# A two-layer trunk on Trainium2: products in pairs in the MLP steps, another bank group for an output projection's last tiles, and a gather moved by nine matmuls

## The chip, the cores and the metric

The kernel runs on one core of one Trainium2 chip. The core has a matmul engine (PE, TensorE), whose weight loads are shown apart as PEld; a vector engine (DVE); a scalar engine (ACT); GpSimd (POOL); and SyncE (SP), which here only issues DMAs. Matmuls write their sums into PSUM, a memory of eight banks of 128 x 512 floats; everything else lies in SBUF. Each engine works through its own list of instructions in order and waits on semaphores for the others. The metric is device time in microseconds (us).

## What is computed

The reference is a trunk of two layers on 512 tokens of width 1024: a latent-attention mixer (MLA) and its MLP, then a gated linear attention mixer (GLA) and its MLP, and a last RMSNorm:

```python
h = xn @ w_in ...                       # mixer: MLA in layer 0, GLA in layer 1
x = x + mixer(rms_norm(x)) @ w_o        # w_o: 1024 x 1024
hid = jnp.square(jax.nn.relu(xn @ w_up))    # w_up: 1024 x 4096
x = x + hid @ w_down                    # w_down: 4096 x 1024
```

All is float32. GLA normalises each head's output (`rms_norm(o, g_norm)`), multiplies by a gate, and projects with `w_o`.

## The kernel before

**Split products.** A float32 product is made of three matmuls on parts: each operand is split into a high and a low part, and the sum of high x high, high x low and low x high is taken (`mm3`, L112 to L114, and the loops of `up_product` and `down_product`). For a weight, ACT writes the high half (tile `wh`, L104) and DVE subtracts it for the low half (`wl`, L107). Both have four buffers, so a product's halves can be written when the product four earlier has ended.

**The MLP (`mlp`).** The 4096 hidden columns are taken in eight blocks of 512. Each block's two large products are done by a scheme of seven products instead of eight (Strassen's, in Winograd's form): quadrants of weights and of data are added and subtracted first, seven products are made, and their sums are combined. `up_first` makes block 0's hidden values. Then `step(b, ...)`, for b = 0 to 6, makes the seven up products of block b + 1 (`up_product`, L946: 24 matmuls of 256 columns) and the seven down products of block b (`down_product`, L955: 12 matmuls of 512 columns), by turns. With U for up and D for down, and the names used in this document, the order before is

```
U11 D11a U21 D12a  T2 D11b T1 D22 U22 D12 T3 D5 T4 D21
```

T1 to T4 and U.. are up products; `D11b` is the one with minus q11, `D22` that with q22, `D12` that with q12; `D5` and `D21` go through `onto`. The sums lie in four single banks "u" for up products, and in two pairs of banks "d" and "e" for down products. `begun` (L964) copies d into e on ACT, so that a further product can be added there; `onto` copies a running sum into a pair of banks (L976), adds a product and copies it back (L978); `add` (L971) adds a finished pair to a running sum on DVE; `finish` (L849, L850) applies the squared ReLU. After a product, `after(name)` fetches the next weight of a name: SP issues a plain DMA (L933, or L134 for the 1 MB tiles `wraw`), POOL one that accumulates (L935). The order of instructions on each engine follows from the order in which the code records them; a scheduler moves instructions of DVE and ACT within it.

**The output projections (`out_start`, `out_proj`).** Eight tiles m = 0 to 7 of 128 output columns are made from eight inputs k. The banks are shared out as two "a", three "b" and three "c". For MLA, tiles 0 and 1 are begun early in the a banks; for GLA, tiles 0, 1, 2 are begun in one b, one c and one a bank. The rest goes through `bank("ac"[c % 2])` with c the pair of tiles, so that tiles 6 and 7 are in c. DVE adds each tile to the residual `xT` (L790). The MLP that follows lays its own banks u, d and e over the same eight.

**The GLA gather (`heads`, `gather`).** When heads 2 and 3 are normalised (`head_norm`: ACT L1552, DVE L1554), `out_start(w_o, Y, 4, "bca")` makes the first four k of three tiles, 36 matmuls. Then `gather(2)` and `gather(3)` transpose each head: per half a head four 128 x 128 transposes on PE (L129) into a c bank, read by ACT (L1564) and, after it, DVE (L1565). One of the three c banks is held by the begun tile, so the third half's transposes need the bank of the first.

Of the kernel before, what the change touches and what calls it, by code (L numbers as in the profile page):

```python
# [14 lines left out]
AF = mybir.ActivationFunctionType  # L15
ALU = mybir.AluOpType
AX = mybir.AxisListType

P = 128
# [3 lines left out]
ND = D // P  # L23
# [27 lines left out]
def trunk_kernel(ctx: ExitStack, tc: tile.TileContext, t_in: dict, out: bass.AP):  # L51
    nc = tc.nc
    PE, ACT, DVE, POOL, SP = nc.tensor, nc.scalar, nc.vector, nc.gpsimd, nc.sync
# [22 lines left out]
    def bank(tag):  # L76
        return psum["pool"].tile([P, 512], F32, tag=f"ps_{tag}", bufs=psum["banks"][tag], name=uname("ps"))
# [11 lines left out]
    def tmp(shape=(P, 512), dt=F32):  # L89
        return sb.tile(list(shape), dt, tag="tmp", bufs=6, name=uname("tmp"))  # L90
# [18 lines left out]
    def mm3(psum, w, x, start, stop):  # L109
        wh, wl = w  # L110
        xh, xl = x
        PE.matmul(psum, wh, xh, start=start, stop=False)  # L112
        PE.matmul(psum, wh, xl, start=False, stop=False)  # L113
        PE.matmul(psum, wl, xh, start=False, stop=stop)  # L114
# [28 lines left out]
    def piece(raw, a, n, order=lambda i: i, at=W_AT):  # L143
        hi = room_for("wh", a, n, at)
        lo = room_for("wl", a, n, at)
        split(raw, hi, lo, order=order)
        return hi, lo

    def cut(pair, *idx):
        return tuple(t[idx] for t in pair)  # L150
# [618 lines left out]
    def out_start(w2d, X, n, tags="aa"):  # L769
        raws, w, ps_ = [], [], []  # L770
        for m, tag in enumerate(tags):
            if m % 2 == 0:
                raws.append(col_chunk(w2d, m * P, 256))
            w.append(piece(raws[-1][:, :, m % 2 * P : (m % 2 + 1) * P], ND, P))
            ps_.append(bank(tag))

        def mms(ks):
            for k in ks:
                for p, w_ in zip(ps_, w):
                    mm3(p, cut(w_, slice(None), k), X[k], k == 0, k == ND - 1)  # L780

        mms(range(n))
        return ps_, raws, lambda: mms(range(n, ND))

    def out_proj(w2d, X, nxt, begun=None):
        ps_, raws, rest = begun or out_start(w2d, X, 0)
        rest()

        def add(m, p):
            DVE.tensor_tensor(xT[m], p, xT[m], ALU.add)  # L790
            nxt.add(m, xT[m])

        for m, p in enumerate(ps_):
            add(m, p)
        for c in range(len(ps_) // 2, ND // 2):
            raw = raws[c] if c < len(raws) else col_chunk(w2d, c * 256, 256)
            tiles = range(max(2 * c, len(ps_)), 2 * c + 2)
            done = [(piece(raw[:, :, m % 2 * P : (m % 2 + 1) * P], ND, P), bank("ac"[c % 2])) for m in tiles]
            for w, p in done:
                a_type(p, w, X)  # L800
            for m, (w, p) in zip(tiles, done):
                add(m, p)


    def mlp(layer, nrm, nxt=None):
        w_up, w_dn = t_in["mlp_w_up"][layer], t_in["mlp_w_down"][layer]
        X = nrm.out
        NB = FF // FB
# [13 lines left out]
        S11, S12, SU, S21, S5 = sums  # L822
# [135 lines left out]
        def step(b, q, r, after):  # L958
            opening = b == 0 and nxt is not None
            (q11, q12), (q21, q22) = q  # L960

            def begun(src):
                t = two_banks("e")
                ACT.activation(t, src, AF.Copy)  # L964
                return t

            def add(total, t):
                if opening:
                    ACT.activation(total, t, AF.Copy)
                else:  # L970
                    DVE.tensor_tensor(total, t, total, ALU.add)  # L971

            def onto(tag, total, a, parts, fresh=False):
                t = two_banks(tag)
                if not fresh:
                    ACT.activation(t, total, AF.Copy)  # L976
                down_product(t, a, parts, fresh)
                ACT.activation(total, t, AF.Copy)  # L978

            A1, A2, s1 = W["A1"], W["A2"], W["S1"]  # L980
            a11, a12, s3, a22 = A1[:, :KH], A1[:, KH:], A2[:, :KH], A2[:, KH:]
            d11, d12, ds1, ds3, d22 = (W[n] for n in ("d11", "d12", "dS1", "dS3", "d22"))

            z = bank("u")
            up_product(z, a11, "11", True)
            y = bank("u")
            ACT.activation(y, z, AF.Copy)

            d = two_banks("d")
            down_product(d, d11, parts_of_quad(q11), True)  # L990
            if opening:
                ACT.activation(S11, d, AF.Copy)
            e = two_banks("e") if opening else begun(d)

            up_product(y, a12, "21", False)
            finish(y, 0, 0, r)
            DVE.tensor_tensor(a11, s1, a11, ALU.add)

            down_product(e, d12, parts_of_quad(q21), opening)
            DVE.tensor_tensor(S11, e, S11, ALU.add)  # L1000
            DVE.tensor_tensor(d11, ds1, d11, ALU.add)
            DVE.tensor_tensor(q12, q22, q12, ALU.subtract)
            DVE.tensor_tensor(q11, q11, q12, ALU.add)

            up_product(z, a11, "T2", False)
            u = tmp()
            ACT.activation(u, z, AF.Copy)
            DVE.tensor_tensor(a12, a11, a12, ALU.add)

            down_product(d, d11, parts_of_quad(q11, -1.0), False)  # L1010
            e = begun(d)
            DVE.tensor_tensor(d12, d11, d12, ALU.add)
            after("d11")

            w = bank("u")
            up_product(w, s1, "T1", True)
            w2 = bank("u")
            ACT.activation(w2, w, AF.Copy)
            after("S1")

            down_product(e, d12, parts_of_quad(q22), False)
            add(S12, e)
            after("d12")

            up_product(w, a12, "22", False)
            c = tmp()
            DVE.tensor_tensor(c, w, u, ALU.add)
            finish(c, 0, 1, r)
            after("A1")

            down_product(d, ds3, parts_of_quad(q12), False)
            add(SU, d)
            after("dS3")
            DVE.tensor_tensor(q22, q22, q11, ALU.subtract)

            up_product(z, s3, "T3", False)
            v = tmp()
            ACT.activation(v, z, AF.Copy)
            c = tmp()
            DVE.tensor_tensor(c, w2, v, ALU.add)  # L1040
            finish(c, 1, 1, r)

            onto("e", S5, ds1, parts_of_quad(q22, -1.0), b == 0)
            after("dS1")
            DVE.tensor_tensor(q21, q21, q11, ALU.subtract)

            up_product(z, a22, "T4", False)
            finish(z, 1, 0, r)
            after("A2")

            onto("d", S21, d22, parts_of_quad(q21, -1.0), opening)
            after("d22")

        up_first(Q[0])
        quadrants()
# [148 lines left out]
    def gla(layer, nrm, vtag, ytag):  # L1204
# [377 lines left out]
        def heads():  # L1582
            for h in (0, 2):
                while any(i not in qk for i in (h, h + 1, 4 + h, 5 + h)):
                    yield
                late = None
                for two in zip(levels(h), levels(h + 1)):
                    for stage in two:
                        products = stage()
                        if late:  # L1590
                            late()
                        late = products
                        yield
                late()
                yield
                while h // 2 not in vdone:
                    yield

                def run(*stages):
                    for stage, r in stages:  # L1600
                        stage(r)
                        yield

                if h == 0:
                    while 0 not in gdone:
                        yield
                    yield from run((states, 0), (own_tiles, 0), (states, 1), (own_tiles, 1), (past, 0), (gated, 0))
                    gates(2)
                    yield from run((past, 1), (gated, 1))
                    gates(3)  # L1610
                else:
                    yield from run((states, 2), (own_tiles, 2), (past, 2), (states, 3))
                    while 1 not in gdone:
                        yield
                    yield from run((gated, 2), (own_tiles, 3), (past, 3), (gated, 3))
                yield from run((head_norm, h), (head_norm, h + 1))
                if h:
                    begun.append(out_start(w_o, Y, 4, "bca"))
                yield from run((gather, h), (gather, h + 1))

        begun = []
        gates(0)
# [128 lines left out]
```

## Time and profile before

| what | value |
|---|---|
| median of 3 runs | 1054.07 us (1053.84 to 1054.35) |
| profiled execution | 1054.16 us |
| its span | 1052.4 us, granted clock 0.999 |
| PE busy | 1043.0 us, 99% |
| DVE busy | 874.2 us, 83% |
| ACT busy | 702.6 us, 67% |
| POOL busy | 113.8 us, 11% |
| share of PE in the chain that ended last | 93% |

The profiled execution's time includes what lies around its span. A line L946 in a row is line 946 of the kernel before; in the kernel after, the same code stands three to some thirty lines further down (L949 for L946, L958 for L955, L793 for L790). A duration in a PE row is from a matmul's start to its modelled end, and matmuls overlap; how fast they follow one another is read from the differences of start times. In the rows a name left of `<-` is written and names right of it are read.

### The profile page before, as it was taken

To read this page: it belongs to the slowest core of one execution; us is meant where nothing else is said; L and a number is where in the kernel's file an instruction comes from. 1 tells how busy PE (TensorE), PEld (TensorE's weight loads), DVE (VectorE), ACT (ScalarE), POOL (GpSimd) and SP (SyncE) were. 2 spreads that over 40 slices of the span, in tenths; PEclk is the share of its full clock that TensorE was granted. 3 is DMA by queue.
4 is the path that set the end of the run, shared out by engine and by line. 5 is a ranking of instruction groups with operands and counts; after the bars stand their busy time and mean duration, and the time that the engine had idled before them with its cause. 6 is when DMAs were issued, how large, how long until landed. Compare 5 with 4: busy or idle time off the path is not lost.

```text
span 1052.4 us, 15648 instructions
## 1 busy us (share of the span) xinstructions
PE 1043.0 (99%) x5966; PEld 910.3 (86%) x5966; DVE 874.2 (83%) x1340; ACT 702.6 (67%) x1074; POOL 113.8 (11%) x128
## 2 busy tenths in 40 slices
PE   9999999999999999999999999999999999999997
PEld 7788888899999999998888888888889999999985
DVE  7889977979889889988687399469889989989983
ACT  8667654677777777776445565555667777777784
POOL 7400010301101011000000000000010010110000
PEclk9999999999999999999999999999999999999999
DMA  7401234776975875843212222164496696696612
GB/s 232 121 21 41 81 100 141 236 189 147 230 198 141 222 214 134 214 160 121 70 62 80 90 72 78 46 161 154 96 249 135 185 247 144 178 244 158 172 61 80
DMA packets 120492, 149.97 MB, mean 143 GB/s; under 512 B 9344, under 2 KB 86144, under 8 KB 120288
## 3 DMA queue, kind: packets, MB, share of 16 engines
q1 hardware_dynamic: 95920, 117.76, 35.3%
q0 software_dynamic: 22400, 29.36, 17.2%
q10 hardware_dynamic: 2096, 1.84, 0.6%
q8 instruction: 47, 0.77, 0.3%
q14 instruction: 29, 0.24, 0.1%
HBM read 144.49 MB, written 4.19 MB: 141 GB/s over the span
## 4 chain that ended last, share of the span: by engine, by line
PE 93%; DVE 3%; ACT 2%; DMA 1%; issue 1%; ACTq 0%; SPq 0%; DVEq 0%
PE ps L955 26%; PE ps L946 26%; PE ps L112 10%; PE ps L114 10%; PE ps L113 10%; PE ps L1140 2%; PE ps L1395 1%; PE ps L129 1%; PE ps L1175 1%; PE ps L414 1%; PE ps L1522 1%; DVE wl L107 1%; DVE acc L245 0%; PE ps L1445 0%; PE ps L677 0%
## 5 line engine op out<-in xcount | busy, mean ns | idle before, releaser
L955 PE MATMUL ps<-wh,set 128*128 128x512 f32 x784 | 259.2, 392 | 0.1
L104 ACT ACTIVATE wh<-wraw 128x1024 fp32r<-128x1024 f32 x139 | 147.0, 1061 | 115.2 <-PE ps L946 40.0
L107 DVE TENSOR_TENSOR wl<-wraw,wh 128x1024 fp32r<-128x1024 f32 x139 | 169.9, 1222 | 40.7 <-ACT wh L104 40.3
L955 PEld LDWEIGHTS ps<-wh,set 128*128 128x128 f32 x784 | 147.1, 188 | 29.3 <-ACT set L104 0.5
L946 PE MATMUL ps<-T,wh 128*128 128x256 f32 x896 | 159.8, 279 | 0.0
L107 DVE TENSOR_TENSOR wl<-comb,wh 128x1024 fp32r<-128x1024 f32 x112 | 136.6, 1219 | 22.8 <-ACT wh L104 22.8
L955 PE MATMUL ps<-wl,set 128*128 128x512 f32 x392 | 153.7, 392 | 0.0
L946 PEld LDWEIGHTS ps<-T,wh 128*128 128x128 f32 x896 | 140.4, 188 | 4.7
L104 ACT ACTIVATE wh<-comb 128x1024 fp32r<-128x1024 f32 x112 | 117.7, 1051 | 25.0 <-PE ps L955 15.0
L946 PE MATMUL ps<-T,wl 128*128 128x256 f32 x448 | 124.9, 279 | 0.0
L946 PE MATMUL ps<-set,wh 128*128 128x256 f32 x672 | 119.7, 280 | 0.0
L112 PE MATMUL ps<-set,wh 128*128 128x512 f32 x280 | 109.2, 391 | 0.5 <-ACT set L1564 0.3
L113 PE MATMUL ps<-set,wh 128*128 128x512 f32 x280 | 109.5, 391 | 0.0
L114 PE MATMUL ps<-set,wl 128*128 128x512 f32 x280 | 109.2, 390 | 0.0
L946 PEld LDWEIGHTS ps<-set,wh 128*128 128x128 f32 x672 | 105.2, 188 | 3.5
L946 PE MATMUL ps<-set,wl 128*128 128x256 f32 x336 | 93.8, 279 | 0.0
L946 PEld LDWEIGHTS ps<-T,wl 128*128 128x128 f32 x448 | 84.2, 188 | 0.1
L955 PEld LDWEIGHTS ps<-wl,set 128*128 128x128 f32 x392 | 73.6, 188 | 11.7
L935 POOL DMA_DIRECT2D comb<-in_mlp_w_down_dram x28 | 33.8, 1207 | 387.9 <-DMA comb<-in_mlp_w_down_dram 271.5
L946 PEld LDWEIGHTS ps<-set,wl 128*128 128x128 f32 x336 | 63.2, 188 | 0.0
L112 PEld LDWEIGHTS ps<-set,wh 128*128 128x128 f32 x280 | 52.5, 188 | 11.6 <-issue 0.6
L114 PEld LDWEIGHTS ps<-set,wl 128*128 128x128 f32 x280 | 52.6, 188 | 10.8
(396 smaller groups left out, 2026.1 us busy)
## 6 DMA issues: line engine op xcount, KB each, us to landing
comb<-in_mlp_w_down_dram SPq DMA_DIRECT2D x74, 512.0 KB, 5.6
wraw<-in_mlp_w_up_dram SPq DMA_DIRECT2D x32, 1024.0 KB, 7.0
comb<-in_mlp_w_down_dram POOLq DMA_DIRECT2D x28, 512.0 KB, 7.6
wraw<-in_gla_w_in_dram SPq DMA_DIRECT2D x12, 1024.0 KB, 5.2
comb<-in_mlp_w_up_dram SPq DMA_DIRECT2D x14, 512.0 KB, 4.4
comb<-in_mlp_w_up_dram POOLq DMA_DIRECT2D x14, 512.0 KB, 10.7
wraw<-in_mlp_w_up_dram POOLq DMA_DIRECT2D x14, 512.0 KB, 6.5
wraw<-in_mla_w_o_dram SPq DMA_DIRECT2D x4, 1024.0 KB, 4.9
```

The costliest lines, as they stand in the source:

```text
L104: order(ACT.activation(hi, src, AF.Copy))
L107: lo_eng.tensor_tensor(lo, src, f(hi), ALU.subtract)
L112: PE.matmul(psum, wh, xh, start=start, stop=False)
L113: PE.matmul(psum, wh, xl, start=False, stop=False)
L114: PE.matmul(psum, wl, xh, start=False, stop=stop)
L129: PE.transpose(psum, src, ident[: src.shape[0], : src.shape[0]])
L414: PE.matmul(p, w[:, i, j * P : (j + 1) * P], x, start=start, stop=stop)
L935: POOL.dma_start(t, q(b, *more), accum_op=ALU.add)
L946: PE.matmul(o, a_, x_, start=start and j == 0 and k == 0 and n == 0, stop=k == KH - 1 and n == 2, skip_group_check=True)
L955: PE.matmul(o, x_, w_, start=start and k == 0 and n == 0, stop=k == 1 and n == 2, skip_group_check=True)
L1140: PE.matmul(p, a, x, start=False, stop=k == 3 and n == 2, skip_group_check=True)
L1175: PE.matmul(o, a, b_, start=False, stop=k == 3 and n == 2, skip_group_check=True)
```

## The change

In the MLP the products of a step become small functions, and the order in which they are called is written down. Step 0 keeps its order. Steps 1 to 6 have

```
U11 D11a U21 D12a  D11b T2 T1 D22 D12 U22 T3 D5 D21 T4      (b = 1 to 5)
U11 D11a U21 D12a  D11b T2 T1 D22 D12 U22 T3 D5 T4 D21      (b = 6)
```

In `out_proj` the last pair of tiles takes "b" instead of "c". In the GLA mixer only three k are made before `gather(2)`; the nine matmuls of the fourth k stand between `gather(2)` and `gather(3)`.

```diff
-        def mms(ks):
-            for k in ks:
+        taken = [0]
+
+        def mms(n=ND):
+            for k in range(taken[0], n):
                 for p, w_ in zip(ps_, w):
                     mm3(p, cut(w_, slice(None), k), X[k], k == 0, k == ND - 1)
+            taken[0] = n
-        mms(range(n))
-        return ps_, raws, lambda: mms(range(n, ND))
+        mms(n)
+        return ps_, raws, mms
...
-            done = [(piece(raw[:, :, m % 2 * P : (m % 2 + 1) * P], ND, P), bank("ac"[c % 2])) for m in tiles]
+            done = [(piece(raw[:, :, m % 2 * P : (m % 2 + 1) * P], ND, P), bank("acab"[c])) for m in tiles]
...
+            part = {"e": e}
+
+            def down_11():
+                down_product(d, d11, parts_of_quad(q11, -1.0), False)
+                part["e"] = begun(d)
+                DVE.tensor_tensor(d12, d11, d12, ALU.add)
+                after("d11")
+
+            def up_t2():
+                up_product(z, a11, "T2", False)
+                u = part["u"] = tmp()
+                ACT.activation(u, z, AF.Copy)
+                DVE.tensor_tensor(a12, a11, a12, ALU.add)
...
+            if b == 0:
+                order = up_t2, down_11, up_t1, down_22, up_22, down_12, up_t3
+            else:
+                order = down_11, up_t2, up_t1, down_22, down_12, up_22, up_t3
+            ends = (up_t4, down_21) if b in (0, NB - 2) else (down_21, up_t4)
+            for product in (*order, down_5, *ends):
+                product()
...
                 if h:
-                    begun.append(out_start(w_o, Y, 4, "bca"))
-                yield from run((gather, h), (gather, h + 1))
+                    begun.append(out_start(w_o, Y, 3, "bca"))
+                yield from run((gather, h))
+                if h:
+                    begun[0][2](4)
+                yield from run((gather, h + 1))
```

The other products' functions hold the lines that stood in the step before, each with its own `after(...)`.

DVE in step b = 2 of the first MLP, before. `wl_656`, `wl_658` and `wl_661` are the low halves for D12a, T2 and D11b:

```order
L107 TENSOR_TENSOR wl_656_3251<-comb_626_3044,wh_655_3250 128x1024
L1003 TENSOR_TENSOR set_481_2162<-set_481_2162,set_482_2163 128x512
L107 TENSOR_TENSOR wl_658_3271<-wraw_623_3023,wh_657_3270 128x1024
L835 SCALAR_TENSOR_TENSOR set_490_2171<-set_481_2162,set_489_2170 128x512
L1012 TENSOR_TENSOR comb_626_3044<-comb_618_2988,comb_626_3044 128x1024
L107 TENSOR_TENSOR set_492_2173<-set_484_2165,set_491_2172 128x512
L107 TENSOR_TENSOR wl_661_3304<-comb_618_2988,wh_660_3303 128x1024
```

The same place now, where `wl_658` is the low half for D11b and `wl_662` that for T2:

```order
L838 SCALAR_TENSOR_TENSOR set_490_2171<-set_481_2162,set_489_2170 128x512
L107 TENSOR_TENSOR set_496_2177<-set_483_2164,set_495_2176 128x512
L1013 TENSOR_TENSOR comb_621_3009<-comb_618_2988,comb_621_3009 128x1024
L107 TENSOR_TENSOR wl_658_3273<-comb_618_2988,wh_657_3272 128x1024
L1020 TENSOR_TENSOR wraw_626_3045<-wraw_626_3045 128x1024
L107 TENSOR_TENSOR set_492_2173<-set_484_2165,set_491_2172 128x512
L107 TENSOR_TENSOR wl_662_3295<-wraw_626_3045,wh_661_3294 128x1024
```

D11b's split moved ahead of T2's, and the addition that prepares a later product's weight (L1008, now L1020) stands between them.

PE where MLA's projection ends and the MLP begins, before. `ps_470` is the projection's tile 7, `ps_502` and `ps_503` are the first two u banks of the MLP, and the names in brackets are the engines that are waited for:

```order
L114 MATMUL ps_470_2065<-set_436_1862,wl_469_2062 128x512
L112 MATMUL ps_502_2189<-set_438_1894,wh_498_2181 128x512 [waits DVE_49,Activation_49]
L113 MATMUL ps_502_2189<-set_438_1894,wh_498_2181 128x512
L114 MATMUL ps_502_2189<-set_438_1894,wl_499_2182 128x512
L112 MATMUL ps_503_2190<-set_438_1894,wh_500_2185 128x512 [waits DVE_49,Activation_49]
L113 MATMUL ps_503_2190<-set_438_1894,wh_500_2185 128x512
L114 MATMUL ps_503_2190<-set_438_1894,wl_501_2186 128x512
```

The same place now:

```order
L114 MATMUL ps_470_2065<-set_436_1862,wl_469_2062 128x512
L112 MATMUL ps_502_2189<-set_438_1894,wh_498_2181 128x512 [waits DVE_49,Activation_49]
L113 MATMUL ps_502_2189<-set_438_1894,wh_498_2181 128x512
L114 MATMUL ps_502_2189<-set_438_1894,wl_499_2182 128x512
L112 MATMUL ps_503_2190<-set_438_1894,wh_500_2185 128x512 [waits Activation_49]
L113 MATMUL ps_503_2190<-set_438_1894,wh_500_2185 128x512
L114 MATMUL ps_503_2190<-set_438_1894,wl_501_2186 128x512 [waits DVE_49]
```

The first matmul into `ps_503` no longer waits for DVE (which there read tile 7 of the projection); the low half `wl_501` is now waited for by itself.

PE at the GLA gather, before. `ps_1249`, `ps_1252`, `ps_1255`, `ps_1258` are the four halves' banks, `ps_1241`, `ps_1244`, `ps_1248` the three begun tiles:

```order
L114 MATMUL ps_1248_6955<-set_1129_6369,wl_1247_6952 128x512
L129 MATMUL ps_1249_6992<-ident_64,g1_6602 128x128 [waits DVE_49]
L129 MATMUL ps_1249_6992<-ident_64,g1_6602 128x128 [waits Activation_49]
L129 MATMUL ps_1249_6992<-ident_64,g1_6602 128x128 [waits DVE_49]
L129 MATMUL ps_1249_6992<-ident_64,g1_6602 128x128 [waits Activation_49]
L129 MATMUL ps_1252_7001<-ident_64,g1_6602 128x128 x4
L112 MATMUL ps_1241_6943<-set_1250_6997,wh_1239_6939 128x512 [waits Activation_49]
L112 MATMUL ps_1244_6948<-set_1250_6997,wh_1242_6944 128x512
L112 MATMUL ps_1248_6955<-set_1250_6997,wh_1246_6951 128x512
L129 MATMUL ps_1255_7010<-ident_64,g1_6602 128x128 [waits DVE_49]
L129 MATMUL ps_1255_7010<-ident_64,g1_6602 128x128 x3
```

The same place now, from the second half's transposes on:

```order
L129 MATMUL ps_1252_6992<-ident_64,g1_6602 128x128 x4
L112 MATMUL ps_1241_6943<-set_1129_6369,wh_1239_6939 128x512
L113 MATMUL ps_1241_6943<-set_1130_6370,wh_1239_6939 128x512
L114 MATMUL ps_1241_6943<-set_1129_6369,wl_1240_6940 128x512
L112 MATMUL ps_1244_6948<-set_1129_6369,wh_1242_6944 128x512
L113 MATMUL ps_1244_6948<-set_1130_6370,wh_1242_6944 128x512
L114 MATMUL ps_1244_6948<-set_1129_6369,wl_1243_6945 128x512
L112 MATMUL ps_1248_6955<-set_1129_6369,wh_1246_6951 128x512
L113 MATMUL ps_1248_6955<-set_1130_6370,wh_1246_6951 128x512
L114 MATMUL ps_1248_6955<-set_1129_6369,wl_1247_6952 128x512
L129 MATMUL ps_1255_7010<-ident_64,g1_6602 128x128 [waits DVE_49]
L129 MATMUL ps_1255_7010<-ident_64,g1_6602 128x128 [waits Activation_49]
```

The nine matmuls on `set_1129` and `set_1130` (the fourth k) moved from ahead of the transposes to between the second and the third set; the third set still waits for DVE.

More of the change, by code (lines that the diff above doesn't have):

```diff
@@ L1003, in step @@
             DVE.tensor_tensor(q11, q11, q12, ALU.add)
[L1005 to L1052, printed above, removed]
+            part = {"e": e}
@@ new lines, in down_11, with up_t1 @@
+            def down_11():
[8 more added lines that the diff above has]
+                DVE.tensor_tensor(a12, a11, a12, ALU.add)
+            def up_t1():
+                w = part["w"] = bank("u")
+                up_product(w, s1, "T1", True)
+                w2 = part["w2"] = bank("u")
+                ACT.activation(w2, w, AF.Copy)
+                after("S1")
@@ new lines, in down_22, with down_12, up_22 @@
+            def down_22():
+                e = part["e"]
+                down_product(e, d12, parts_of_quad(q22), False)
+                add(S12, e)
+                after("d12")
+            def down_12():
+                down_product(d, ds3, parts_of_quad(q12), False)
+                add(SU, d)
+                after("dS3")
+                DVE.tensor_tensor(q22, q22, q11, ALU.subtract)
+            def up_22():
+                w = part["w"]
+                up_product(w, a12, "22", False)
+                c = tmp()
+                DVE.tensor_tensor(c, w, part["u"], ALU.add)
+                finish(c, 0, 1, r)
+                after("A1")
@@ new lines, in up_t3, with down_5, down_21 @@
+            def up_t3():
+                up_product(z, s3, "T3", False)
+                v = tmp()
+                ACT.activation(v, z, AF.Copy)
+                c = tmp()
+                DVE.tensor_tensor(c, part["w2"], v, ALU.add)
+                finish(c, 1, 1, r)
+            def down_5():
+                onto("e", S5, ds1, parts_of_quad(q22, -1.0), b == 0)
+                after("dS1")
+                DVE.tensor_tensor(q21, q21, q11, ALU.subtract)
+            def down_21():
+                onto("d", S21, d22, parts_of_quad(q21, -1.0), opening)
+                after("d22")
@@ new lines, in up_t4 @@
+            def up_t4():
+                up_product(z, a22, "T4", False)
+                finish(z, 1, 0, r)
+                after("A2")
+            if b == 0:
[5 more added lines that the diff above has]
+                product()
```

## The prediction

> **What bounds the kernel now.** I read the busy times first, then the chain that ended last, then the busy time by stretch (columns: window, its length, busy us and instructions of PE, PEld, DVE, ACT, POOL, granted clock, DMA share, GB/s).
>
> ```profile
> PE 1043.0 (99%) x5966; PEld 910.3 (86%) x5966; DVE 874.2 (83%) x1340; ACT 702.6 (67%) x1074; POOL 113.8 (11%) x128
> ...
> PE 93%; DVE 3%; ACT 2%; DMA 1%; issue 1%; ACTq 0%; SPq 0%; DVEq 0%
> PE ps L955 26%; PE ps L946 26%; PE ps L112 10%; PE ps L114 10%; PE ps L113 10%; PE ps L1140 2%; PE ps L1395 1%; PE ps L129 1%; PE ps L1175 1%; PE ps L414 1%; PE ps L1522 1%; DVE wl L107 1%; DVE acc L245 0%; PE ps L1445 0%; PE ps L677 0%
> ```
> ```profile
> 206.00:479.00 273.00, 272.97 (x1768) 248.18 (x1767) 240.90 (x268) 201.54 (x251) 32.24 (x27) 1.00 0.71 180
> 749.00:1023.00 274.00, 273.95 (x1781) 249.19 (x1780) 245.00 (x273) 203.98 (x254) 30.05 (x24) 1.00 0.69 172
> ```
>
> PE never rests: 99% of the span, 93% of the chain, and 272.97 of 273.00 us in the first MLP at full clock. The change leaves every matmul in place, so it can win only what stands between matmuls, or lose by starving PE. DVE is next: 240.90/273 = 88% in the first MLP and 89% in the second, so its order matters. "Busy" for PE is pipelined occupancy, so turns from one kind of product to the other don't show in it; start to start they do.
>
> **Term A: the order of products in the MLP steps.** An up product (L946) is 24 matmuls of 256 columns, a down product (L955) 12 of 512. The next rows are from the chain in order of time (start, length, matmuls), and the last two from the timeline of a long run of 512-column matmuls.
>
> ```profile
> 212.32 5.37 PE ps L946 x46
> 218.69 5.03 PE ps L955 x22
> 223.71 2.80 PE ps L946 x24
> ...
> 284.80 2.80 PE ps L946 x24
> 287.60 2.75 PE ps L955 x12
> ...
> 473.61 2.80 PE ps L946 x24
> ```
> ```profile
> 483.27 0.39 PE L1140 MATMUL ps<-set,wl 128*128 128x512 f32 x1
> ...
> 490.75 0.39 PE L1140 MATMUL ps<-set,wl 128*128 128x512 f32 x1
> ```
>
> From 223.71 to 473.61 the two kinds alternate: 45 pairs in 249.90 us, 5.553 us a pair. Without a turn: the x46 row is two up products in a row, 5.37/46 = 0.1167 each, so 24 take 2.802. Between the two L1140 rows lie 33 matmuls: 7.48/33 = 0.2267 each, so 12 take 2.720 (the x22 row, two down products in a row, has 5.03 against 22 × 0.2267 = 4.99, so the border between two of a kind costs nearly nothing). A pair without turns is 5.522; alternation costs 0.031 a pair, the turn into a kind and out of it.
>
> In steps 1 to 6 of each MLP the order becomes up, down, up, down down, up up, down down, up up, down down, and the last up product meets the next step's first (step 6 ends up, down). That is 84 runs of one kind before and 50 after: 34 fewer, or 17 pairs of turns an MLP, 34 in both. 34 × 0.032 (0.031 rounded up by the L955 row at 287.60, where 2.75 − 2.72 is already 0.03) = 1.09 us. Bounds: nothing, if it is not the alternation that costs; 34 × 0.040 = 1.4 by the x22 row's own excess.
>
> What must hide it: nothing is added or dropped on any engine. In steps 1 to 5 three down products begin one up product earlier and three up products one down product later (two of each in step 6). The tightest parts I find for the first kind are those of the down product with minus q11 (`D11b`), fifth in step 2 and later:
>
> ```profile
> 289.44 1.22 DVE L107 TENSOR_TENSOR wl<-wraw,wh 128x1024 fp32r<-128x1024 f32 x1
> ...
> 292.91 1.22 DVE L107 TENSOR_TENSOR wl<-comb,wh 128x1024 fp32r<-128x1024 f32 x1
> ```
> ```profile
> 301.85 1.01 ACT L964 ACTIVATE ps<-ps 128x1024 f32<-128x1024 f32 x1
> ```
>
> The low half of its weight ends at 294.13; it started at 284.80 + 2.80 + 2.75 + 2.80 + 2.75 + 2.80 = 298.70. If DVE did it at the same time, the cover would shrink from 4.57 to 1.77 us; but DVE's order now has this split three rows sooner, ahead of the one at 289.44 (for `T2`, which goes back). Its ACT copy from bank pair d to e (ends 302.86) was wanted after one up product, now after two. The last two down products, which are seeded by an ACT copy into a bank pair that an earlier one frees, keep their distance to it: two up products and a down product lie between, before and after. The weights' DMAs move by one product (SP now puts the `dS3` slot's fetch before that of the 1 MB `A1`), against landing times of 5.6 and 7.0 us in the page's DMA rows:
>
> ```profile
> L104 ACT ACTIVATE wh<-wraw 128x1024 fp32r<-128x1024 f32 x139 | 147.0, 1061 | 115.2 <-PE ps L946 40.0
> ...
> comb<-in_mlp_w_down_dram SPq DMA_DIRECT2D x74, 512.0 KB, 5.6
> wraw<-in_mlp_w_up_dram SPq DMA_DIRECT2D x32, 1024.0 KB, 7.0
> ```
>
> `A1` is asked for after the up product with q22, now one 2.75 us product later: from its end to the next step's first product lie T3, two down products and T4, 11.1 us (13.9 before). Less 7.0 to land, 1.06 for ACT's copy and 1.22 for DVE's low half, 1.8 us are left. So these moves cost nothing in the sum; POOL's order is the same.
>
> [...] The trace has 5.553 against 5.522 us. [...]
>
> **Term B: the last two tiles of an output projection in bank group b.** Timeline at the end of the attention layer's projection; the matmul with the wait is the first that writes the second u bank of the MLP's first products, where tile 7 of the projection lay.
>
> ```profile
> 184.13 0.69 DVE L790 TENSOR_TENSOR xT<-ps,xT 128x512 f32<-128x512 f32 x1 [0.52 <-PE ps L114]
> ```
> ```profile
> 184.38 0.39 PE L114 MATMUL ps<-set,wl 128*128 128x512 f32 x1
> 184.97 0.47 PE L112 MATMUL ps<-set,wh 128*128 128x512 f32 x1 [0.20 <-DVE xT L790]
> ...
> 186.43 0.39 PE L112 MATMUL ps<-set,wh 128*128 128x512 f32 x1
> ```
>
> From 184.38 to 186.43 are 7 spacings (six matmuls lie between): 2.05 − 7 × 0.2267 = 0.46 us. PE waits until DVE's addition ends at 184.82, then runs some wide spacings. In the changed order this matmul no longer waits for DVE, only the low half of a weight two rows on does, which DVE writes sooner than that addition. So the whole 0.46 goes; bounds 0 (another wait takes over) and 0.46, and I take the upper one since that weight's half stands ahead of the addition on DVE. The GLA layer's end shows no such stall: nothing there.
>
> **Term C: the gather of the GLA heads.** Before, PE runs 36 matmuls, 16 transposes (x8, x4, x4), with matmuls between the last ones.
>
> ```profile
> 684.31 0.61 DVE L1554 TENSOR_SCALAR g<-g,srstd 128x256 f32<-128x256 f32 x2
> ...
> 688.79 1.41 DVE L1565 SCALAR_TENSOR_TENSOR set<-ps,gains,set 128x512 fp32r<-128x512 f32 x2 [1.91 <-ACT set L1564]
> ```
> ```profile
> 685.39 0.39 PE L112 MATMUL ps<-set,wh 128*128 128x512 f32 x1
> ...
> 687.21 0.39 PE L114 MATMUL ps<-set,wl 128*128 128x512 f32 x1
> 687.44 1.03 PE L129 MATMUL ps<-ident,g 128*128 128x128 f32 x8
> 688.81 0.98 PE L112 MATMUL ps<-set,wh 128*128 128x512 f32 x3 [0.34 <-ACT set L1564]
> 689.63 0.63 PE L129 MATMUL ps<-ident,g 128*128 128x128 f32 x4
> ...
> 693.55 0.39 PE L113 MATMUL ps<-set,wh 128*128 128x512 f32 x1
> ```
> ```profile
> 686.26 0.91 ACT L1552 ACTIVATE g<-g,srstd 128x256 f32<-128x256 f32 x2 [0.66 <-DVE srstd L291]
> 688.07 1.26 ACT L1564 ACTIVATE set<-ps,gains 128x512 fp32r<-128x512 f32 x2 [0.90 <-PE ps L129]
> ```
>
> From 687.21 to 693.55 lie 17 matmul spacings (3.85) and 16 transposes of about 0.109 (1.03 for eight less the last one's tail: 1.74); 6.34 − 5.59 = 0.74 us of waits and restarts. After, the first eight transposes stand where the 28th matmul did, at 685.39; head 2 is ready by then (DVE ends 684.92). They end about 686.27, and the nine matmuls of the fourth part cover to 688.31. The third set of transposes wants the first set's bank, freed by DVE L1565, which follows ACT L1564. ACT's order still has the two L1552 first, ending 687.17; then 0.63 for L1564, 0.75 for L1565 and 0.1 to PE give about 688.65 to 688.70. PE waits 0.35 to 0.4 and loses 0.1 at the restart: 0.5. Gain 0.74 − 0.5 = 0.24; bounds 0 (PE stalls as long) and 0.74 (no stall).
>
> **The sum.** 1.09 + 0.46 + 0.24 = 1.79 us. The profiled execution took 1054.16 around its span of 1052.4, 0.09 above the median of 1054.07; 1054.16 − 1.79 = 1052.37, and against the median 1052.3. With 0.2% (2.11 us) as about what a measurement of this kernel tells from no change, the border to "faster" is 1051.96, near.
>
> **Rivals.**
> - *The gather's wait goes altogether.* If the first bank comes free 0.4 us sooner (ACT taking L1564 before the second L1552), C is 0.74: sum 2.29, 1051.8, faster. For: the matmuls put in between cover 2.04 us. Against: ACT's order has both L1552 ahead.
> - *The order of products is worth nothing.* If the 0.031 a pair belongs to a product's own start (its first weights, its bank) and not to the turn, A is 0: sum 0.70, 1053.4, the same. For: each product begins with new weights. Against: x46 and x22, where like follows like at steady pace. [...]
> - *The bank only exchanges the wait.* B = 0: sum 1.33, 1052.7.
> - *DVE comes late for the products that moved ahead*, slower. DVE is busy 88%; `D11b`'s low half has 1.77 us cover if DVE does not follow. Twelve steps (six an MLP) would each stall by x; slower than 0.2% needs 12x = 2.11 + 1.79 = 3.9, so x above 0.33 us, that is the split ending 2.1 us later than before relative to PE. At 0.5 us: 1052.3 + 6 = 1058.3. For: twelve repeats of any small miss. Against: the order puts this split sooner. The same price holds for ACT copies that guard a bank.
>
> **How the numbers follow.** All three terms about as worked out: 0.64, own range 1051.8 to 1052.6 (C from 0 to 0.74, A by ±0.2), two fifths of it under 1051.96. Gather without a wait 0.12 (1051.8); no gain from the order 0.08 (1053.4); bank exchanged 0.03 (1052.7); DVE or ACT late 0.13, in my eyes above 1056. Faster: 0.4 × 0.64 + 0.12 = 0.38; same: 0.38 + 0.08 + 0.03 = 0.49; slower 0.13. The range 1051.6 to 1053.5 leaves out the slow case and a little below.
>
> **What would show it.** Right: in the chain of the changed kernel, x24 + x24 + two x12 take 11.07 us where two pairs took 11.11; the wait of L112 on L790 is gone from the waits; at the GLA gather one wait of PE L129 on DVE L1565 of about 0.4 us. Wrong: a wait of L958 or L949 (the new lines of the products) on ACT or DVE repeated by step, which would lengthen both MLPs beyond 273.

## The result, and the profile after

The kernel after took 1052.12 us (median of 12 runs) beside 1054.26 us for the kernel before (12 runs). The medians differ by 2.14 us; the ratio of 0.9983, with a 95% interval of 0.9976 to 0.9990, stands for 1.8 us, with an interval of 1.1 to 2.5. The profiled execution's span fell from 1052.4 to 1050.4 us. It is a faster kernel, by about 0.2%.

The head of the profile of the kernel after, and its two MLP windows:

```profile
PE 1040.9 (99%) x5966; PEld 909.7 (87%) x5966; DVE 874.3 (83%) x1340; ACT 699.3 (67%) x1074; POOL 113.9 (11%) x128
```
```profile
206.00:479.00 273.00, 272.97 (x1775) 248.80 (x1774) 241.96 (x270) 201.03 (x253) 32.25 (x27) 1.00 0.72 181
749.00:1023.00 274.00, 273.95 (x1779) 249.59 (x1779) 244.39 (x273) 202.33 (x254) 30.06 (x24) 1.00 0.68 171
```

The number of matmuls, 5966, is the same and PE's busy share is still 99%. These views show nothing of where 2 us went, since PE is busy for 272.97 of the first MLP's 273.00 us both before and after. The differences of start times do. In the chain in order of time, an MLP step of the kernel after reads (start, length, matmuls):

```profile
253.86 5.47 PE ps L958 x24
259.34 5.60 PE ps L949 x48
264.94 5.47 PE ps L958 x24
270.41 5.60 PE ps L949 x48
276.01 5.47 PE ps L958 x24
```

Two down products and two up products take 5.47 + 5.60 = 11.07 us, where two alternating pairs took 11.11. The list of PE's waits holds four entries, and the wait of L112 on the projection's addition and that on the gather's L1564 are gone:

```profile
PE ps L1687 <- DVE ones L174: 1.2, 1, 1.2
PE ps L414 <- ACT set L255: 1.1, 1, 1.1
PE ps L670 <- ACT pr L123: 0.2, 1, 0.2
PE ps L1420 <- DVE A L1432: 0.2, 1, 0.2
```

In this list no product of an MLP waits for ACT or DVE. To see where the time went, I took the start times of the same matmuls in both traces and subtracted:

| stretch on PE | before, us | after, us | difference |
|---|---|---|---|
| span's start to 150 matmuls ahead of the first MLP step's first product | 172.14 | 172.18 | +0.04 |
| those 150 matmuls (the end of MLA's projection and the MLP's first products) | 34.47 | 34.01 | -0.46 |
| first MLP, its first step product to the end of its last | 272.39 | 271.83 | -0.56 |
| from there through the GLA mixer to the second MLP's steps | 270.17 | 269.87 | -0.30 |
| second MLP | 274.51 | 273.90 | -0.61 |
| the rest | 28.69 | 28.59 | -0.10 |
| sum (the span) | 1052.37 | 1050.38 | -1.99 |

The stretch with the gather is seen closer in three timelines of the kernel after, one for each of PE, ACT and DVE:

```profile
684.24 0.39 PE L114 MATMUL ps<-set,wl 128*128 128x512 f32 x1
684.47 1.03 PE L129 MATMUL ps<-ident,g 128*128 128x128 f32 x8
685.26 0.48 PE L112 MATMUL ps<-set,wh 128*128 128x512 f32 x1
...
687.19 0.39 PE L114 MATMUL ps<-set,wl 128*128 128x512 f32 x1
687.67 0.66 PE L129 MATMUL ps<-ident,g 128*128 128x128 f32 x4
```
```profile
685.34 0.91 ACT L1577 ACTIVATE g<-g,srstd 128x256 f32<-128x256 f32 x2 [0.66 <-DVE srstd L291]
686.16 1.25 ACT L1589 ACTIVATE set<-ps,gains 128x512 fp32r<-128x512 f32 x2
```
```profile
686.86 1.41 DVE L1590 SCALAR_TENSOR_TENSOR set<-ps,gains,set 128x512 fp32r<-128x512 f32 x2 [0.90 <-ACT set L1589]
```

ACT reads the first transposed half only after the two scalings of the last head (686.16), DVE follows at 686.86, and the third set of transposes starts at 687.67, 0.48 us after the matmul ahead of it where 0.227 is the pace: 0.25 us late. The rest lies at the transposes: the third set's x4 row takes 0.66 us where the fourth set's, at 688.40, takes 0.60, and the eight spacings from 685.26 to 687.19 take 1.93 us where 1.81 is the pace; eight transposes and the step to the next matmul, 0.79 us (684.47 to 685.26) where 0.87 is the pace, give some of it back. In all, the 16 transposes and the matmuls among them lose 0.39 us against the steady pace, where they lost 0.74 before.

### The profile page after: what moved, and what is told of

Read it like the earlier page. It is cut to its first block, busy times and chain, and to the rows that moved or that the text cites. A ratio compares the mean times of both kernels' runs of the same rounds, so it can differ in the third digit from the quotient of the medians.

```text
span 1050.4 us, 15641 instructions
## 1 busy us (share of the span) xinstructions
PE 1040.9 (99%) x5966; PEld 909.7 (87%) x5966; DVE 874.3 (83%) x1340; ACT 699.3 (67%) x1074; POOL 113.9 (11%) x128
## 4 chain that ended last, share of the span: by engine, by line
PE 93%; ACT 3%; DVE 2%; DMA 1%; issue 0%; ACTq 0%; SPq 0%; DVEq 0%
PE ps L949 26%; PE ps L958 26%; PE ps L112 10%; PE ps L114 10%; PE ps L113 10%; PE ps L1165 2%; PE ps L1420 1%; PE ps L129 1%; PE ps L1200 1%; PE ps L414 1%; PE ps L1547 1%; DVE wl L107 1%; PE ps L1470 0%; PE ps L677 0%; ACT wh L104 0%
## 5 line engine op out<-in xcount | busy, mean ns | idle before, releaser
L958 PE MATMUL ps<-wh,set 128*128 128x512 f32 x784 | 252.9, 391 | 0.1
L112 PE MATMUL ps<-set,wh 128*128 128x512 f32 x280 | 109.5, 391 | 0.0
```

Source lines behind the costliest of these rows:

```text
L958: PE.matmul(o, x_, w_, start=start and k == 0 and n == 0, stop=k == 1 and n == 2, skip_group_check=True)
```

## The experiments

My theory was the prediction's: three terms that don't depend on one another (turns between kinds of product, one bank, one gather), with enough cover on DVE and ACT. The rivals to be told apart were that the order of products gains nothing by itself, that the bank only exchanges a wait, that DVE is near to being late, and, within the first term, what about a turn costs time. Where nothing else is said, a code cut shows the edit against the kernel after; `...` stands for lines or arguments left out.

**The order alone (a_only).**

```diff
-            done = [(piece(...), bank("acab"[c])) for m in tiles]
+            done = [(piece(...), bank("ac"[c % 2])) for m in tiles]
...
-                    begun.append(out_start(w_o, Y, 3, "bca"))
-                yield from run((gather, h))
-                if h:
-                    begun[0][2](4)
-                yield from run((gather, h + 1))
+                    begun.append(out_start(w_o, Y, 4, "bca"))
+                yield from run((gather, h), (gather, h + 1))
```

> The paired order of products in steps 1 to 6 alone; the last tiles' bank and the gather as before. If each turn between up and down products costs 0.03 us: each MLP (first up product to the end of the last down product) 0.55 us shorter than before, two pairs of products in a row 11.07 us instead of 11.11, the whole kernel about 1.1 us faster than before; the wait on the projection's tile 7 (0.2 us, 0.46 with what follows) and the gather's stall (0.74) are still there. If the MLPs gain only together with the other parts, they stay at 272.4 and 274.5 us.

It took 1053.26 us beside 1054.23: a ratio of 0.9989, interval 0.9979 to 0.9998, which stands for 1.2 us (the medians differ by 0.97). The MLPs took 271.85 and 273.92 us, 0.54 and 0.59 less than before; the step's rows in the chain are those of the kernel after, and both other stalls are in PE's waits:

```profile
254.63 5.47 PE ps L958 x24
260.11 5.60 PE ps L949 x48
```
```profile
PE ps L112 <- ACT set L1589: 0.3, 1, 0.3
...
PE ps L112 <- DVE xT L793: 0.2, 1, 0.2
```

So the order gains by itself, and what it gains in the two MLPs of this trace is 0.54 + 0.59 = 1.13 us.

**The bank alone (b_only)** and **the gather alone (c_only).** Both have the old order of products in every step (`if True: order = up_t2, ...` and `ends = (up_t4, down_21)`); the first has the old gather, the second the old bank.

> The last pair of an output projection's tiles in bank group b alone. If it takes the wait away: no wait of the MLP's first products on the projection's addition, first layer's projection to MLP 0.46 us shorter, both MLPs as before (272.4, 274.5 us). If it only exchanges the wait, another of 0.2 us or more stands within the MLP's first products.

> Three k ahead of the gather and the fourth between its two heads, alone. If the gain is the cover of the nine matmuls less a wait for the first half's bank: what is lost at the gather goes from 0.74 to about 0.4 us, and a wait of the third set of transposes on DVE is there. Nothing else moves.

With the bank alone the last 150 matmuls ahead of the MLP's steps took 34.01 us (34.47 before) and the MLPs 272.44 and 274.50. In every kernel with the new bank that stretch took 34.01, and in every one with the old bank 34.45 to 34.47; the timeline of b_only where PE had stood still shows the steady 0.227 (three spacings in 0.68 us):

```profile
184.38 0.39 PE L113 MATMUL ps<-set,wh 128*128 128x512 f32 x1
...
185.06 0.39 PE L113 MATMUL ps<-set,wh 128*128 128x512 f32 x1
```

With the gather alone its loss was 0.39 us (0.74 before), and the third set of transposes came 0.25 us late, as in the kernel after. The whole times (one run each, 1053.86 and 1054.33 us beside 1054.23) can't tell 0.3 to 0.5 us: in the trace of c_only the 399th matmul, long ahead of every change, starts 87.06 us after the span's start, in that of the kernel before 86.50.

**What a turn costs (narrow_down).** This is the kernel before (the edit is against it), with two matmuls of 256 columns in place of each of 512 in a down product.

```diff
-                        PE.matmul(o, x_, w_, start=start and k == 0 and n == 0, ...)
+                        for i in range(2):
+                            PE.matmul(o[:, i * TH : (i + 1) * TH], x_, w_[:, i * TH : (i + 1) * TH], ...)
```

> The kernel before with every down product's 512-column matmuls as two of 256 columns (24 matmuls a product, the same sums), so that up and down products alternate at one width. If the turn costs because the width changes, the excess goes: a pair takes 48 x 0.1167 = 5.60 us. If the turn costs because another kind of product starts (other tiles, other banks), the 0.031 stays: 5.63 us a pair.

Neither number came: a pair took 2.81 + 2.87 = 5.68 us (the chain), because the 256-column matmuls of a down product ran at 0.120 us each, those of an up product at 0.1167. In the timeline of one such product:

```profile
279.40 0.40 PE L956 MATMUL ps<-wh,set 128*128 128x256 f32 x2
279.63 0.40 PE L956 MATMUL ps<-wl,set 128*128 128x256 f32 x2
279.87 0.64 PE L956 MATMUL ps<-wh,set 128*128 128x256 f32 x4
...
280.59 0.64 PE L956 MATMUL ps<-wh,set 128*128 128x256 f32 x4
...
282.03 0.40 PE L956 MATMUL ps<-wh,set 128*128 128x256 f32 x2
```

From 280.59 to 282.03 are 12 matmuls, 0.120 each, not 0.1167. Against that pace a pair without any turn would take 24 × 0.120 + 24 × 0.1167 = 5.68, which is what it took: there is no excess, and the first four matmuls (279.40 to 279.87, 0.1175 each) are not slow. In the kernel after, a run of down products begins otherwise:

```profile
253.70 0.40 PE L958 MATMUL ps<-wh,set 128*128 128x512 f32 x1
253.93 0.40 PE L958 MATMUL ps<-wl,set 128*128 128x512 f32 x1
254.17 0.62 PE L958 MATMUL ps<-wh,set 128*128 128x512 f32 x2
254.63 0.39 PE L958 MATMUL ps<-wl,set 128*128 128x512 f32 x1
254.86 0.61 PE L958 MATMUL ps<-wh,set 128*128 128x512 f32 x2
```

Its first five matmuls take 254.86 − 253.70 = 1.16 us where five at 0.2267 take 1.133: 0.027 of a turn's cost lie there, and some 0.008 in the last spacing before the up products. A second down product behind the first has no such start: an x24 row of 5.47 us is 0.03 above 24 × 0.2267. In these products the cost sits behind the step from narrow to wide matmuls. This run can't say more: why the narrow down product has the pace 0.120, and so whether another effect hides in it, stays open.

The trace of the kernel before adds to this. Where PE goes from one loop's matmuls to another's at 512 columns (L1140 to L112, other weights and a new sum), the pace stays: from 503.18 to 505.90 lie 12 spacings, 2.72 us, 0.2267 each.

```profile
503.18 0.39 PE L1140 MATMUL ps<-set,wh 128*128 128x512 f32 x1
...
504.31 0.39 PE L112 MATMUL ps<-set,wh 128*128 128x512 f32 x1
...
505.90 0.39 PE L113 MATMUL ps<-set,wh 128*128 128x512 f32 x1
```

So a new kind of product by itself did not cost there. But the step in width does not account for it alone either. Two more places of that trace show this:

```profile
37.91 0.39 PE L112 MATMUL ps<-wh,set 128*128 128x512 f32 x1
38.38 0.47 PE L464 MATMUL ps<-set,mean_q 128*96 128x512 f32 x1
38.69 0.39 PE L113 MATMUL ps<-wl,set 128*128 128x512 f32 x1
...
39.85 0.39 PE L112 MATMUL ps<-wh,set 128*128 128x512 f32 x1
```
```profile
671.22 0.28 PE L114 MATMUL ps<-set,ktl 128*128 128x256 f32 x1
671.34 0.39 PE L112 MATMUL ps<-wh,set 128*128 128x512 f32 x1
...
672.47 0.39 PE L114 MATMUL ps<-wh,set 128*128 128x512 f32 x1
```

Behind a pause (37.91 to 38.38), with 512 columns on both sides, the five spacings from 38.69 to 39.85 take 1.16 us, as at the start of a run of down products. Behind 256 columns at 671.34, five spacings take 1.13 us, the steady pace. In these two places a change of width was neither needed for the slow start (1.16 us with 512 columns on both sides) nor enough for it (1.13 us behind 256); what brings it about stays open.

**How much cover DVE has (dve6, dve12, dve12_old).** The kernel after, with additions of q11 to itself into an unused tile, put on DVE in steps 1 to 6 (six a step in dve6, twelve in dve12 and dve12_old; dve12_old has the old order of products as well).

```diff
             DVE.tensor_tensor(q11, q11, q12, ALU.add)
+            if b:
+                for _ in range(6):
+                    DVE.tensor_tensor(extra, q11, q11, ALU.add)
```

> The kernel after with six more 128x512 additions on DVE in each of steps 1 to 6, put behind the update of q11 and ahead of the low half of the weight of the down product with minus q11; about 3.6 us of DVE a step, beside some 5 us that DVE has free in a step. If the cover of the moved products is some microseconds, PE shows no new wait and the MLPs keep their lengths within 0.3 us. If the cover is thin (1.8 us), PE waits in each of the twelve steps, and the MLPs grow by about 6 x 1 to 6 x 2 us each.

> The same with twelve additions, about 7.3 us of DVE a step. More than the free 5 us: DVE becomes the bound in steps 1 to 6, waits on DVE at the products, and the MLPs grow by some 2 to 3 us a step, 12 to 18 us each. If they don't grow, DVE has more room than its busy share says.

> Twelve additions on DVE in steps 1 to 6 as in dve12, but with the order of products of the kernel before in those steps. If DVE as a whole is the bound then, each MLP grows by about as much as in dve12 (18 us). If the paired order had less cover for the products that moved ahead, the old order grows clearly less, by 12 us or under.

With six, the MLPs took 271.85 and 273.95 us, as without, and PE had no new wait, although DVE's busy time in the first MLP rose to 95% of the window:

```profile
206.00:479.00 273.00, 272.98 (x1774) 248.74 (x1773) 259.80 (x304) 200.17 (x252) 31.22 (x25) 1.00 0.71 181
```

With twelve, they took 290.36 and 292.67 us, 18.5 and 18.8 more, and PE waited at the products (dve12, PE's waits):

```profile
PE ps L958 <- ACT set L837: 12.4, 10, 1.7
PE ps L949 <- DVE wl L107: 9.8, 12, 1.7
```

With twelve and the old order, they took 289.58 and 292.57 us. The old order without additions took 272.44 and 274.50 (b_only), so it pays 17.1 and 18.1 us where the paired order pays 18.5 and 18.8. The scheduler spread the additions among the split products' halves, in step 2 of dve12 from 292.8 to 310.4 us. The edge lies between six and twelve additions a step, 3.6 and 7.2 us of DVE work at the 0.60 us that one takes in the chain of dve12 (292.87, L1009). The expectations had some 5 us free in a step; in the window of the kernel after, 273.00 − 241.96 = 31.0 us are, 4.4 in each of seven steps. Past it the paired order has lost its gain: its MLPs are 0.8 and 0.1 us longer than those of the old order, in one run each.

**Pairs in step 0 as well (pairs0).**

```diff
-            if b == 0:
+            if False:
                 order = up_t2, down_11, up_t1, down_22, up_22, down_12, up_t3
...
-            ends = (up_t4, down_21) if b in (0, NB - 2) else (down_21, up_t4)
+            ends = (up_t4, down_21) if b == NB - 2 else (down_21, up_t4)
```

> The kernel after with the paired order in step 0 as well (the last step's end as it is). By 0.032 us a turn, 0.15 to 0.2 us less for each MLP if nothing waits; against it, the first step has no time between the first products and the fetch and split of the first weights, so a wait of 0.5 us or more at the first down product that moves ahead would make it slower.

The MLPs took 272.34 and 274.40 us, 0.5 more each than in the kernel after: the gain of four runs of one kind fewer is lost to a wait. It is not at a down product but at the up product T2's low half, in the timeline of PE:

```profile
214.47 0.39 PE L949 MATMUL ps<-T,wh 128*128 128x256 f32 x2
215.44 0.38 PE L949 MATMUL ps<-T,wl 128*128 128x256 f32 x1 [0.58 <-DVE wl L107]
```

In step 0 PE runs most of T2 right behind U21, ahead of `D12a`, in this kernel, in the kernel before and in the kernel after: the scheduler moves PE's instructions there too, not only those of DVE and ACT. But DVE's splits follow the order of the calls there. In the kernel after T2's low half starts at 210.73; in pairs0 the one for D11b takes that place, and T2's starts at 214.16, behind a wait for ACT's high half:

```profile
214.16 1.23 DVE L107 TENSOR_TENSOR wl<-wraw,wh 128x1024 fp32r<-128x1024 f32 x1 [1.17 <-ACT wh L104]
```

PE, which ran T2 first all the same, had to wait for it.

**The gather without its last wait (late_spread, late_spread_t).** The last head's scaling is recorded after the first head's gather, and nine matmuls stand between the last head's two halves.

```diff
-                yield from run((head_norm, h), (head_norm, h + 1))
+                yield from run((head_norm, h))
+                if not h:
+                    yield from run((head_norm, h + 1))
...
                     begun[0][2](4)
-                yield from run((gather, h + 1))
+                    yield from run((head_norm, h + 1))
+                    gather(h + 1, (0,))
+                    begun[0][2](5)
+                    gather(h + 1, (1,))
+                    begun[0][2](6)
```

> The kernel after with the norm of the last head recorded after the gather of the one before, so that ACT reads the first transposed half between the two scalings of the last head, and with nine matmuls of the projection between the last head's two halves as well. If the gather's wait is for the first half's bank behind ACT's scalings, it goes: what is lost at the gather falls from 0.39 to about 0.15 us, 0.25 us faster than the kernel after. If PE restarts cost as much as the wait did, it stays at 0.3 to 0.4.

The loss at the gather fell to 0.15 us, and the stretch from MLP to MLP to 269.57 us (269.87 after). The third set of transposes follows the matmul ahead of it at the steady pace:

```profile
687.42 0.39 PE L114 MATMUL ps<-set,wl 128*128 128x512 f32 x1
687.65 0.60 PE L129 MATMUL ps<-ident,g 128*128 128x128 f32 x4
688.00 0.48 PE L112 MATMUL ps<-set,wh 128*128 128x512 f32 x1
688.32 0.40 PE L113 MATMUL ps<-set,wh 128*128 128x512 f32 x1
...
690.17 0.60 PE L129 MATMUL ps<-ident,g 128*128 128x128 f32 x4
```

ACT now reads the first half before the last head's second scaling, which starts at 686.57:

```profile
685.99 0.67 ACT L1589 ACTIVATE set<-ps,gains 128x512 fp32r<-128x512 f32 x1
```

The third set stands ahead of the matmuls that were spread between the last head's halves, so it is the move of the scaling that took its wait away. Of the 0.15 us left, little lies at the restart itself: four transposes and the step to the next matmul take 0.35 us (687.65 to 688.00) where four at 0.109 take 0.44 (of the x8 row's 1.03 us in the kernel after, 0.27 are one transpose; the rest is seven spacings), and the matmul after that comes 0.31 us later instead of 0.227, so the two nearly cancel. Most of it lies in the spacings behind: the eight from 688.32 to 690.17 take 1.85 us, where 1.81 is the pace. Timed beside the kernel after on one chip:

> The kernel after once more, beside the next one on the same chip: about 1.8 to 2.1 us faster than before, a ratio of 0.998.

> The kernel after with the gather's last wait gone (as in the run late_spread), timed: 0.25 us less than the kernel after by the trace, a ratio to before of 0.9978 against 0.998; the two intervals will overlap.

The kernel after had a ratio of 0.9982 (0.9973 to 0.9991), 1052.27 us beside 1054.37; the one with the gather's last wait gone had 0.9977 (0.9968 to 0.9986), 1052.17 us. The intervals overlap, and the spans of the four traces (1050.4 and 1050.6 us for the kernel after, 1050.4 and 1050.5 for this one) do not tell them apart. What is shown is that the gather's stretch is 0.25 us shorter in both traces; that the kernel as a whole is faster is not shown.

## Why the prediction was right

The forecast was 1052.3 us with a range of 1051.6 to 1053.5, and "within 0.2%" as the likeliest of the three; 1052.12 lies in the range, and a ratio of 0.9983 is within 0.2%. By the medians the gain is 0.20%, on the border to "faster". That the time came so near is in part luck: the forecast was worked out from 1054.07 us for the kernel before, which took 1054.26 in this comparison, and the gain was larger than the sum's 1.79 us (1.99 between the two traces).

- **Term A, 1.09 us.** The traces of before and after give 0.56 + 0.61, the order alone 0.54 + 0.59. The rows foretold, 11.07 us for two and two products, came. The count of 34 pairs of turns and the price of 0.032 held (1.13 / 34 = 0.033); what in a turn costs it is open. That the moves cost nothing also held. The prediction gave the low half for D11b 1.77 us of cover if DVE kept its time. DVE did not: in step 2 of the kernel after this half ends at 290.77, and D11b, the second of the two down products in the chain's row, starts at about 292.64 + 5.47/2 = 295.4, 4.6 us later, as much as the 4.57 before.

```profile
289.55 1.22 DVE L107 TENSOR_TENSOR wl<-comb,wh 128x1024 fp32r<-128x1024 f32 x1
```
```profile
292.64 5.47 PE ps L958 x24
```

Six further additions on DVE in each step, three of which (1.8 us) stand ahead of that half in step 2 of dve6, still brought no wait.
- **The rival that the order is worth nothing** fell, by the order alone (ratio 0.9989, interval below 1). The steady spacings by themselves, 0.2267 us at 512 columns and 0.1167 at 256, give 5.522 us for a pair in any order (5.553 was taken by turns), and so have no place for the 0.033 us that a pair of turns gained.
- **Term B, 0.46 us.** 34.47 to 34.01 us, 0.46. The bank alone gave the same. No wait took its place.
- **Term C, 0.24 us.** 0.74 to 0.39, a gain of 0.35. The mechanism was right (the first half's bank, behind ACT's two scalings), and the step that failed in size is "PE waits 0.35 to 0.4 and loses 0.1 at the restart: 0.5": PE was 0.25 us late, and the restart cost 0.06 (the x4 rows of 0.66 and 0.60 us). The 0.1 for the restart was an estimate that no run shows. The chain ACT, DVE, PE came out 0.06 to 0.11 us shorter (687.67 − 684.47 = 3.20 us from the first transposes, 3.26 to 3.31 forecast), as ACT's next operation started ahead of the end of the one before (686.16 against 685.34 + 0.91). I had said that the wait would be seen in PE's list of waits. It is not there: measured from the modelled end of the matmul ahead (687.19 + 0.39 = 687.58) to 687.67, PE was idle for only 0.09 us. The rival in which the wait goes altogether had C at 0.74; late_spread, without the wait, still loses 0.15, so it would have been 0.6.
- **The sum.** 1.79 was forecast; the terms measured in the two traces are 0.56 + 0.61 + 0.46 + 0.35 = 1.98, and the spans differ by 1.99. That these agree to 0.01 is chance: outside the terms the table has +0.04 at the start, −0.10 in the rest, and a GLA stretch 0.05 longer than the gather's gain alone would make it.
- **The slow rival, DVE late,** did not come: the limit lies beyond 3.6 us more of DVE work a step (dve6, six additions at 0.60). That it can come is shown by dve12, and, for a first step, by pairs0, which is slower than the kernel after by 0.9 us in its span.

## What to carry to other kernels

PE's busy share was 99% before and after and did not show the 1.99 us between the two spans; the differences of start times against the steady pace of each matmul's width (0.2267 us at 512 columns, 0.1167 at 256) did. Putting products of one width next to one another gained 0.033 us a pair of turns here, where the work that feeds them ran ahead (the low half for D11b by 4.6 us in step 2); in the first step, where the splits came in another order than PE took the products, it lost 0.5 us an MLP. As a step in width cost nothing at another place of this kernel (671.34, five spacings in 1.13 us), measure the price in your own trace first. For a bank that waits to be freed, look at what stands ahead of the reader in its own engine's queue: moving ACT's read ahead of one scaling took 0.25 us off the gather, after the nine matmuls in front had taken 0.35.

## What the runs showed that was not expected

Matmuls of 256 columns have a steady pace of 0.120 us each in the split down products, 0.1167 in the up products; splitting the down products cost 6.3 us in each MLP (272.39 to 278.73, 274.51 to 280.82). Why one width has two paces was not tried. And DVE's busy time in the first MLP's window rose from 89% to 95% (dve6) while the MLPs took 271.85 and 273.95 us, beside 271.83 and 273.90; PE was busy for 272.98 of that window's 273.00 us.
